# GpSimd's second parts of weight units: four instructions of 256 columns instead of one of 1024

## The chip, the core and the metric

The kernel runs on one core of a Trainium2 chip. The core has a matrix engine (TensorE, PE in the profile; its weight loads are a row of their own, PEld), three elementwise engines (VectorE or DVE, ScalarE or ACT, GpSimd or POOL), and SyncE (SP), which issues the transfers from DRAM. The engines run side by side, each in its own order, and wait for each other by semaphores. The metric is the device time of one launch in microseconds (us).

## The reference, cut to what matters

One layer of a hybrid decoder over 2048 prompt tokens and 32 sample tokens, with 1024 features:

```
h = rmsnorm(x, g_mix); proj = h @ w_in              # 1024 x 2560, split in u, q, k, v, g
ssm = S5 state space of u (scan over tokens, GELU, GLU)
ret = retention of q, k, v, g (4 heads, rotary phases, chunks of 128)
x = x + concat(ssm, ret) @ w_out
x = x + memory_attend(rmsnorm(x, g_xattn), mk, mv, w_mq, w_mo)   # 256 memory tokens, 4 heads
h = rmsnorm(x, g_mlp)
x = x + square(relu(h @ w_up)) @ w_down             # 1024 x 4096 and back
y = rmsnorm(x, g_final)
```

All of it is float32. The memory's keys and values are made from the prompt memory by two further products.

## The kernel before, in words

The tokens are worked on in four blocks of 512 (the second with the 32 sample tokens beside it). Each block goes through the mixers, the output projection, the memory attention and the MLP. Weights stream from DRAM in units of 128 x 1024 float32 numbers (`raw`), over and over, once per block.

A float32 product is made as three products in the faster float32r format. For this each weight unit gets two parts, `whl[:, 0]` (the first part: the number in float32r) and `whl[:, 1]` (the second: what is left), and the activations likewise (`act`, `z`, `actl`). ScalarE makes the first part of a weight unit with a copy. VectorE or GpSimd makes the second part: it subtracts the first part from `raw`. This second part is what the change touches. It is made in the function `lo` inside `split_unit`. Which engine makes it is set by a table (`SET`, read by `ve`) or, for some units, by the smaller of two guesses. Matrix products read the unit in steps of 128 columns or more (`fm`: for each step of 128, the passes first x first, first x second, second x first), so the first product that needs the second part stands two or three places behind the first product of a unit.

The memory's key and value products write `kt` and `vt`; with these two further sets of weights are multiplied in (products named `dn<-kt,whl` and `dn<-whl,vt`), between the first block's mixers and its attention.

The order of instructions is not written out by hand. The class `Order` runs a main sequence of weight units and, in between, chains (state space, retention, norms) as generators. A model of the engines (`Model`, with a start cost and a cost per column for each elementwise engine; 140 ns and 2.11 ns for GpSimd) guesses when each instruction ends, and a chain goes on when the guess says that its inputs are there. So every instruction that is added to an engine moves the guesses, and with them the places at which chains come in between on all engines. All instructions of the elementwise engines pass through one helper, which is why they all have line 197 in the profile; matrix products have line 445, transposes 449.

In the rows below: `pkd`, `psc`, `pkv`, `po` and `pt` are retention's products, `Sv`, `scs`, `kr` and `qr` what they read; `py`, `vr` and `vi` are the state space's products, `Yr`, `Yi` and `t` its scans and their results; `rst`, `rsy` and `parts` are the short chain that makes the reciprocal root of a norm.

Of the kernel before, what the change touches and what calls it, by code (L numbers as in the profile page):

```python
# [18 lines left out]
P = 128  # L19
# [40 lines left out]
class Item:  # L60
    """A piece of the main sequence: a weight unit to load and what to do with it, or a call."""

# [12 lines left out]
class Model:  # L75
    """Guesses when each engine does what it is given, from the operands and the engines' rates."""

# [10 lines left out]
    def where(self, ap):  # L88
        """First and last partition and element, outermost stride, elements within it."""
        dims = [tuple(d) for d in ap.ap]  # L90
        p0 = p1 = 0
        lo = ap.offset
        if ap.space != DRAM:
            row, n = dims.pop(0)
            if row:
                p0, lo = divmod(lo, row)
            p1 = p0 + n
        dims = sorted((abs(s), n) for s, n in dims if n > 1)
        w = 1 + sum((n - 1) * s for s, n in dims[:-1])
        s, n = dims[-1] if dims else (1, 1)  # L100
        return p0, p1, lo, lo + (n - 1) * s + w, s, w
# [81 lines left out]
class Engine:  # L183
    """An engine whose instructions the model sees."""

# [15 lines left out]
class Either:  # L201
    """An instruction for the engine that SET names, or for the one that the model has done with it first."""

# [27 lines left out]
class Order:  # L231
    """Emits the program in the order of the tensor engine's time: a main sequence of weight units,
    and chains that come in between when their latencies have passed."""

# [4 lines left out]
    def spawn(self, gen, *aps):  # L239
        """A chain, from when the tiles are ready."""  # L240
        s = Side(gen, max(self.clock, self.model.ready(*aps)))
        self.sides.append(s)
        return s

    def resume(self, s):
        """A chain goes on when the engines have done what it gave them, or some time later, or when tiles are ready."""
        last, self.model.last = self.model.last, 0.0
        try:
            x = next(s.gen)
            s.last = self.model.last + (SET[x] if isinstance(x, str) else 200)  # L250
            if x is None or isinstance(x, str):
                s.wake = max(self.clock, s.last)
            elif isinstance(x, list):
                s.wake = max(self.clock, self.model.ready(*x))
            else:
                s.wake = max(s.wake, self.clock) + x
        except StopIteration:
            s.done = True
            self.sides.remove(s)
        self.model.last = max(last, self.model.last)  # L260

    def work(self, out, ins, cost):
        """A matrix product."""
        self.clock = max(self.clock, self.model.after("PE", [out], ins)) + cost
        self.model.note("PE", [out], ins, self.clock)
# [63 lines left out]
def tile_decoder_step(ctx: ExitStack, tc: tile.TileContext, ins: dict, outs: dict):  # L329
# [93 lines left out]
    def split_unit(raw, eng, pool=None, tag="whl", bufs=NW):  # L423
        """Both float32r parts of a unit, [P, 2, 1024]."""
        hl = (pool or wpool).tile([P, 2, 1024], F32R, tag=tag, name=tag, bufs=bufs)
        A.activation(hl[:, 0, :], raw, AF.Copy)

        def lo():
            e = eng or min((V, G), key=lambda e: max(model.free[e.key], model.ready(hl)) + 1024 * Model.RATE[e.key][1])
            e.tensor_tensor(out=hl[:, 1, :], in0=raw, in1=hl[:, 0, :].bitcast(F32), op=ALU.subtract)  # L430
        return hl, lo
# [29 lines left out]
    def split(dst, src, scale=None):  # L461
        """dst[:, 0] + dst[:, 1] = src (* scale) in float32r parts."""
        split_first(dst, src, scale)
        split_rest(dst, src, scale)

    def rsqrt(pool, tag, x, n):
        """x ** -0.5 on [P, n]."""
        y = pool.tile([P, n], F32, tag=tag + "y", name="rsy")
# [14 lines left out]
    def fm(w, acts, t, out, nk=KT, order=None):  # L483
        """One 128-row tile of W^T X: w(k, s) gives lhsT; fills out with (PSUM tile, column, columns)."""
        for o, n in pieces(t) if isinstance(t, int) else t:
# [9 lines left out]
    def stats(pool, acc, cols, eps_tag):  # L495
        """(mean square + eps) ** -0.5 by token; cols: list of (lhsT slice of acc, rows, further summands)."""
        n = len(cols)
# [20 lines left out]
    def spread(dst, rs, t, last=None, row=None):  # L518
        """dst[p, token] = rs[token]: rs column i holds tokens i*128.., `last` the sample column; row: space for 512 tokens."""
        nt = min(t, BT) // P  # L520
# [23 lines left out]
    def s5_setup(sp):  # L544
        """The tables and matrices of the state space, four pairs of groups at a time, into DRAM."""
        cnt = [0]
# [26 lines left out]
        def turns(*gens):  # L573
            """One instruction of each in turn."""
            gens, n = list(gens), 0
# [8 lines left out]
        def poly(x, cs, out):  # L584
            """((cs[0] x + cs[1]) x + ...) x, without a constant term."""
            ts(x, cs[0], None, mul, out=out)
            yield
            for c in cs[1:]:
                stt(out, c, x, add, mul, out=out)
                yield  # L590
# [117 lines left out]
        yield from turns(angle(), quadrant(), exp(lr, mag), sine(), cosine(), recip())  # L708
        # a = mag (cos + i sin), and the parts of a product with it
        a, b_ = tt(cst[:, 0:2], both(st_["ev"]), mul), tt(cst[:, 1:3], both(st_["odd"]), mul)  # L710
# [62 lines left out]
        def products(out, n, x, y, tab, neg):  # L773
            """out gets the real and imaginary parts of (x + i y) tab, the latter with neg for tab."""
            SH = [P, 4, n, 16]
# [51 lines left out]
    def all_tables(jt, fhf, fl, hpi):  # L827
        """cos and sin of the angles' multiples."""
        W = [P, 4, 129]
# [21 lines left out]

    # The sample tokens go with block SB up to the queries, then through the MLP with the next one.
    blk = [dict(b=b, sample=b == SB, t=TM_ if b == SB else BT, c0=b * BT + (NS if b > SB else 0),
# [22 lines left out]
    def fill(side, lst, n):  # L876
        """Runs a chain until lst has n entries."""
        while len(lst) < n and not side.done:
            od.resume(side)

    def fm_item(src, view, acts, t, done, nk=KT, eng=None, order=None, tag="lo"):
        """One weight unit: view(hl) gives a list of w(k, s); done(i, out) takes the i-th result."""
        def fn(hl):
# [14 lines left out]

# [1 line left out]
    M = {}  # L900
# [36 lines left out]
    def mem_items():  # L937
        """Keys and values of the memory, and the query and output weights with them multiplied in."""
        T_ = {"k": [], "v": []}
# [71 lines left out]

# [1 line left out]
    RING = {"qr": (0, 1), "kr": (2, 3), "cosr": (4,), "sinr": (5,), "rb": (6,), "gate": (7, 10), "tmp": (8, 9),  # L1013
# [30 lines left out]
    def mix_take(B, k, x, rest=None):  # L1044
        """One row tile of the input: its parts and squares; `rest` comes in between."""
        t = B["t"]
# [53 lines left out]
    def first_load(B, units, side):  # L1100
        """The first block's input with the weights of its first product, and a chain in between."""
        B["acts"], xs, raws, hls, half = [], [], [], [], 512
# [424 lines left out]
    def ret_keep(B, h, i, x):  # L1527
        """Sets the sample columns of a query, key or gate tile aside."""
        if B["sample"]:
# [163 lines left out]

# [1 line left out]
    def rk(shape, tag, bufs=1, dt=F32):  # L1695
# [31 lines left out]
    def normed_split(B, o, gain, hs, t):  # L1727
        """Its first part; gives what does the second."""
        hs[o] = a = act() if o < KT - 4 or "rest" not in pool else zact()
# [160 lines left out]
    def sample_keep(B):  # L1890
        """Sets the sample columns of the normalised input aside."""
        M["hss"] = t = rk((P, 2, NB, 2, NS), "pmk", 1, F32R)[:, 0]
# [6 lines left out]
    def sample_items():  # L1899
        """The sample tokens' queries, their attention over the caches, and its output weights."""  # L1900
        held["zps"] = True
# [47 lines left out]
    def sample_rows(Z):  # L1949
        """The sum of both parts of the rows in PSUM, and its transpose, tile by tile."""  # L1950
        ps = Z["ps"]
# [92 lines left out]
    def mo_last(B, u, ahead):  # L2044
        """The last two heads, row tile by row tile."""
        keep = []
# [326 lines left out]
```

## Time and profile before

| | |
|---|---|
| median of 3 runs | 3097.52 us (3088.29 to 3099.51) |
| span of the profiled execution | 3086.3 us |
| PE busy in it | 2950.1 us, 96% |
| DVE busy | 1826.7 us, 59% |
| POOL busy | 1189.3 us, 39% |
| ACT busy | 1005.9 us, 33% |

The profiled execution has only its span, from the first to the last instruction; what a launch takes beside that is not listed for it. The span is 2.0 us under the fastest of the three runs and 11.2 us under their median. A busy matrix engine is not yet one that works at its peak, but idle time of PE is time in which nothing of the main work goes on, and here it is 136 us of the span.

### The profile page before, as it was taken

Reading aid. Unit: us, or ns where it says so; the run is one execution under the profiler, and the core shown is the slowest. Engines: PE = TensorE matmul, PEld = TensorE weight load, DVE = VectorE, ACT = ScalarE, POOL = GpSimd, SP = SyncE. Lnnn points to the kernel's source line nnn. Section 1 sums busy time; section 2 is a strip of 40 time slices with the busy share of each in tenths; the row PEclk is TensorE's granted clock in tenths of the full one; section 3 lists DMA queues with packets and bytes.
Section 4 is the critical chain, followed back from the end, with each engine's and each line's share of the span. In section 5 each row is a group of like instructions: output and inputs, shape, how many; then the busy total and the mean of one; then the engine's idle time right before and its main releaser. Section 6 shows DMA issues by size and latency. Waiting matters only on the chain.

```text
span 3086.3 us, 42360 instructions
## 1 busy us (share of the span) xinstructions
PE 2950.1 (96%) x16676; PEld 2566.3 (83%) x16676; DVE 1826.7 (59%) x3079; ACT 1005.9 (33%) x1440; POOL 1189.3 (39%) x764
## 2 busy tenths in 40 slices
PE   8898899998989999999999999999999999999998
PEld 6788787877877878887987888788999998878887
DVE  9968868679686563334465555655533344554334
ACT  4432232322444332223343333343322223332222
POOL 5424434244454243333524333361523325153333
PEclk9999999999999999999999999999999999999999
DMA  5452252342674322224324444542222233222222
GB/s 150 136 176 97 97 166 96 130 145 72 220 251 157 105 89 96 96 96 140 117 83 138 142 146 147 190 145 89 83 89 89 86 133 119 89 89 96 96 96 75
DMA packets 138950, 374.32 MB, mean 121 GB/s; under 512 B 18656, under 2 KB 39808, under 8 KB 138752
## 3 DMA queue, kind: packets, MB, share of 16 engines
q1 hardware_dynamic: 138176, 371.10, 36.1%
q8 instruction: 131, 2.15, 0.3%
q14 instruction: 67, 0.55, 0.1%
q10 hardware_dynamic: 576, 0.52, 0.1%
HBM read 334.17 MB, written 37.40 MB: 120 GB/s over the span
## 4 chain that ended last, share of the span: by engine, by line
PE 61%; DVE 2%; issue 1%; DMA 1%; ACT 1%; POOL 1%; SPq 0%; POOLq 0%; ACTq 0%; DVEq 0%
PE dn L445 54%; PE sc L445 6%; PE zps L445 1%; DMA raw<-in_w_down 1%; DVE rst L197 1%; ACT whl L197 0%; PE ptp L449 0%; DVE rsy L197 0%; DVE act L197 0%; DVE pmk L197 0%; PE st L445 0%; DVE whl L197 0%; POOL whl L197 0%; POOL act L197 0%; PE sp L445 0%
## 5 line engine op out<-in xcount | busy, mean ns | idle before, releaser
L445 PE MATMUL dn<-act,whl 128*128 128x512 f32 (+2 forms) x4704 | 914.2, 348 | 8.4 <-DVE whl L197 7.4
L445 PE MATMUL dn<-actl,whl 128*128 128x512 f32 (+2 forms) x4656 | 917.3, 356 | 5.1 <-DVE x L197 4.9
L445 PEld LDWEIGHTS dn<-actl,whl 128*128 128x128 f32 x4656 | 767.5, 188 | 134.6 <-issue 3.8
L445 PEld LDWEIGHTS dn<-act,whl 128*128 128x128 f32 x4704 | 753.4, 190 | 116.5 <-DVE whl L197 8.4
L197 POOL TENSOR_TENSOR whl<-raw,whl 128x1024 fp32r<-128x1024 f32 x225 | 559.1, 2487 | 549.1 <-ACT whl L197 536.1
L197 ACT ACTIVATE whl<-raw 128x1024 fp32r<-128x1024 f32 (+1 forms) x505 | 522.7, 1045 | 655.5 <-PE dn L445 445.2
L197 DVE TENSOR_TENSOR x<-dn,x 128x512 f32<-128x512 f32 (+2 forms) x496 | 291.1, 605 | 429.0 <-PE dn L445 428.3
L197 DVE TENSOR_TENSOR whl<-raw,whl 128x1024 fp32r<-128x1024 f32 (+1 forms) x280 | 401.7, 1441 | 165.2 <-ACT whl L197 152.9
L445 PE MATMUL dn<-z,whl 128*128 128x512 f32 (+1 forms) x2160 | 434.9, 353 | 0.0
L445 PEld LDWEIGHTS dn<-z,whl 128*128 128x128 f32 x2160 | 353.7, 188 | 56.8 <-issue 1.1
L197 POOL TENSOR_TENSOR actl<-sq,actl 128x512 fp32r<-128x512 f32 (+1 forms) x128 | 171.3, 1339 | 485.8 <-DVE sq L197 471.5
L197 DVE SCALAR_TENSOR_TENSOR relu<-dn,rb 128x512 f32<-128x512 f32 (+1 forms) x160 | 91.6, 589 | 324.7 <-PE dn L445 317.3
L197 ACT ACTIVATE actl<-relu 128x512 fp32r<-128x512 f32 (+1 forms) x128 | 82.0, 641 | 515.9 <-DVE relu L197 515.9
L445 PE MATMUL dn<-whl,act 128*128 128x512 f32 x768 | 200.1, 408 | 10.8 <-ACT whl L197 6.1
L197 POOL TENSOR_TENSOR acc<-acc,relu 128x512 f32<-128x512 f32 (+2 forms) x77 | 107.4, 1395 | 249.9 <-ACT relu L197 247.8
L445 PEld LDWEIGHTS dn<-whl,act 128*128 128x128 f32 x768 | 165.8, 253 | 34.4 <-ACT whl L197 6.8
L197 DVE TENSOR_TENSOR sq<-relu 128x512 f32<-128x512 f32 (+1 forms) x128 | 90.2, 704 | 14.8 <-POOL actl L197 2.3
L445 PE MATMUL sc<-whl,act 128*128 128x256 f32 x576 | 81.0, 293 | 15.0 <-ACT p L197 9.2
L445 PEld LDWEIGHTS sc<-whl,act 128*128 128x128 f32 x576 | 76.0, 200 | 16.1 <-ACT p L197 9.9
L197 DVE SCALAR_TENSOR_TENSOR act<-x,small,act 128x512 fp32r<-128x512 f32 (+2 forms) x76 | 70.0, 928 | 27.0 <-ACT act L197 26.9
L445 PE MATMUL sc<-whl,z 128*128 128x256 f32 x576 | 80.7, 291 | 0.0
L197 ACT ACTIVATE act<-x,small 128x512 fp32r<-128x512 f32 (+2 forms) x76 | 52.9, 699 | 78.9 <-DVE x L197 55.0
(317 smaller groups left out, 2743.9 us busy)
## 6 DMA issues: line engine op xcount, KB each, us to landing
raw<-in_w_up SPq DMA_DIRECT2D x128, 512.0 KB, 3.5
raw<-in_w_down SPq DMA_DIRECT2D x128, 512.0 KB, 3.5
raw<-in_w_out SPq DMA_DIRECT2D x32, 512.0 KB, 3.5
raw<-wq_d SPq DMA_DIRECT2D x32, 512.0 KB, 3.6
raw<-wo_d SPq DMA_DIRECT2D x32, 512.0 KB, 3.5
x<-in_xT SPq DMA_DIRECT2D x48, 256.0 KB, 4.3
pm<-pm_d SPq DMA_DIRECT2D x16, 768.0 KB, 4.6
tab<-tab_d SPq DMA_DIRECT2D x16, 516.0 KB, 3.5
```

The lines of the kernel that those rows point to most:

```text
L197: return f(*args, **kw)
L445: T.matmul(out, lhsT, rhs, start=start, stop=stop)
```

## The change

`lo` now makes the second part, where GpSimd makes it, in four instructions of 256 columns, one behind the other. VectorE's stay as they were, one of 1024 columns. The choice of engine by guesses is unchanged, and so are the model's rates; the model books each of the four instructions with its own start cost.

```
         def lo():
             e = eng or min((V, G), key=lambda e: max(model.free[e.key], model.ready(hl)) + 1024 * Model.RATE[e.key][1])
-            e.tensor_tensor(out=hl[:, 1, :], in0=raw, in1=hl[:, 0, :].bitcast(F32), op=ALU.subtract)
+            n = 256 if e is G else 1024
+            for i in range(0, 1024, n):
+                e.tensor_tensor(out=hl[:, 1, i:i + n], in0=raw[:, i:i + n], in1=hl[:, 0, i:i + n].bitcast(F32), op=ALU.subtract)
...
```

The rest of the diff takes comments out. Lines behind the change move down by two, so 445 and 449 are 447 and 451 in the changed kernel.

GpSimd's order in the first block, where units stand between retention's `qr` and `kr`, before:

```order
L197 TENSOR_TENSOR qr<-qr,tmp 128x512
L197 TENSOR_TENSOR whl<-raw,whl 128x1024
L197 TENSOR_TENSOR kr<-kr,tmp 128x512
L197 TENSOR_TENSOR whl<-raw,whl 128x1024
L197 TENSOR_TENSOR z<-v_338,jt 128x516
L197 TENSOR_TENSOR pm_135<-cb_678,cb_679 64x4x5x16 x2
```

And the same place now:

```order
L197 TENSOR_TENSOR qr<-qr,tmp 128x512
L197 TENSOR_TENSOR whl<-raw,whl 128x256 x4
L197 TENSOR_TENSOR kr<-kr,tmp 128x512
L197 TENSOR_TENSOR whl<-raw,whl 128x256 x4
L197 TENSOR_TENSOR pm_135<-cb_687,cb_688 64x4x5x16 x2
L197 TENSOR_TENSOR z<-v_339,jt 128x516
```

Each unit is four instructions, `kr` stands behind the four of the unit ahead of it, and one instruction on `z` has left GpSimd for VectorE here.

PE's order where weights are multiplied into the memory's keys (`dn<-kt,whl`), with the semaphores that each product waits for (the engine's name is the semaphore's), before:

```order
L445 MATMUL dn<-kt,whl 128x256 [waits Activation_49]
L445 MATMUL dn<-kt,whl 128x256
L445 MATMUL dn<-kt,whl 128x256 [waits Pool_49]
L445 MATMUL dn<-kt,whl 128x256 x21
L445 MATMUL dn<-kt,whl 128x256 [waits DVE_49,Activation_49]
```

And now:

```order
L447 MATMUL dn<-kt,whl 128x256 [waits Activation_49]
L447 MATMUL dn<-kt,whl 128x256
L447 MATMUL dn<-kt,whl 128x256 [waits Pool_49]
L447 MATMUL dn<-kt,whl 128x256 x2
L447 MATMUL dn<-kt,whl 128x256 [waits Pool_49]
L447 MATMUL dn<-kt,whl 128x256 x11
L447 MATMUL dn<-kt,whl 128x256 [waits Pool_49]
L447 MATMUL dn<-kt,whl 128x256 x6
L447 MATMUL dn<-kt,whl 128x256 [waits DVE_49,Activation_49]
```

The third product waited for the whole second part; now it waits for a quarter of it, and later products wait for later quarters.

PE's order around the first retention head, before:

```order
L445 MATMUL dn<-act,whl 128x512 x72
L449 MATMUL pkd<-ident,kr 128x128 x4
L445 MATMUL psc<-qr,kr 128x128 x4
L445 MATMUL dn<-act,whl 128x512 x12
L445 MATMUL pkv<-tm_520,kd 128x128 x4
L445 MATMUL dn<-act,whl 128x512 x6
L449 MATMUL qt<-ident,tre_133 128x128 x4
L449 MATMUL qt<-ident,tim_134 128x128 x4
L445 MATMUL po<-tm_520,scs 128x128 x2
```

And now:

```order
L447 MATMUL dn<-act,whl 128x512 x75
L451 MATMUL pkd<-ident,kr 128x128 x4
L447 MATMUL psc<-qr,kr 128x128 x4
L447 MATMUL dn<-act,whl 128x512 x12
L447 MATMUL pkv<-tm_523,kd 128x128 x4
L451 MATMUL qt<-ident,tre_133 128x128 x4
L451 MATMUL qt<-ident,tim_134 128x128 x4
L447 MATMUL dn<-act,whl 128x512 x9
L447 MATMUL po<-tm_523,scs 128x128 x2
```

The head's first products come three weight products later, its `po` six later, and the two transposes of the state space's tables (`qt`) three earlier.

## Rows read from the trace of the kernel before

**Rows 1.** The page: span, then busy time, share and instructions of each engine.

```profile
span 3086.3 us, 42360 instructions
PE 2950.1 (96%) x16676; PEld 2566.3 (83%) x16676; DVE 1826.7 (59%) x3079; ACT 1005.9 (33%) x1440; POOL 1189.3 (39%) x764
```

**Rows 2.** Busy time by stretch: start:end length, then PE, PEld, DVE, ACT, POOL, clock, DMA.

```profile
0.00:1100.00 1100.00, 996.40 (x5811) 871.23 (x5812) 856.47 (x1657) 388.22 (x594) 448.51 (x334) 0.98 0.44 141
1100.00:3000.00 1900.00, 1878.62 (x10441) 1629.58 (x10440) 934.21 (x1353) 593.88 (x806) 707.99 (x405) 1.00 0.33 112
3000.00:3086.00 86.00, 75.03 (x427) 65.47 (x425) 36.06 (x71) 23.82 (x41) 32.76 (x26) 0.94 0.23 76
```

**Rows 3.** GpSimd's instructions by shape: count | busy, mean ns | idle before, releasers.

```profile
L197 POOL TENSOR_TENSOR whl<-raw,whl 128x1024 fp32r<-128x1024 f32 x225 | 559.1, 2487 | 549.1 <-ACT whl L197 536.1 <-issue 5.9 <-DMA raw<-in_w_up 3.6
L197 POOL TENSOR_TENSOR actl<-sq,actl 128x512 fp32r<-128x512 f32 x96 | 126.8, 1321 | 364.3 <-DVE sq L197 350.0 <-PE pp L449 10.0 <-DMA x<-cat_d 4.3
L197 POOL TENSOR_TENSOR acc<-acc,relu 128x256 f32<-128x256 f32 x7 | 5.2, 738 | 7.3 <-ACT relu L197 7.1
```

**Rows 4.** GpSimd's instructions, first 1100 us alone, the costliest group.

```profile
L197 POOL TENSOR_TENSOR whl<-raw,whl 128x1024 fp32r<-128x1024 f32 x65 | 162.2, 2497 | 109.2 <-ACT whl L197 103.1 <-issue 5.9
```

**Rows 5.** PE's waits in the first 1100 us: us in total, times, longest.

```profile
PE py L445 <- DVE t L197: 14.1, 9, 3.2
PE pkd L449 <- POOL kr L197: 13.4, 12, 2.1
PE pt L449 <- DVE scs L197: 12.8, 5, 3.9
PE dn L445 <- DVE whl L197: 12.1, 8, 2.2
PE po L445 <- DVE Sv L197: 8.0, 6, 4.0
...
PE dn L445 <- POOL whl L197: 6.5, 6, 2.2
```

**Rows 6.** PE's waits from 800 to 950 us.

```profile
PE dn L445 <- DVE whl L197: 9.2, 6, 2.2
```

**Rows 7.** Order of time, 888 to 893.5 us: start, length, instruction, [idle before, releaser].

```profile
888.79 2.35 POOL L197 TENSOR_TENSOR whl<-tm,whl 128x1024 fp32r<-128x1024 f32 x1 [2.58 <-ACT whl L197]
...
889.31 2.12 DVE L197 TENSOR_TENSOR vt<-wst,vt 128x256 fp32r<-128x256 f32 x1 [0.48 <-ACT vt L197]
...
891.20 1.22 PE L445 MATMUL dn<-kt,whl 128*128 128x256 f32 x4 [1.93 <-POOL whl L197]
```

**Rows 8.** Order of time, 1014 to 1020.5 us.

```profile
1014.86 2.39 POOL L197 TENSOR_TENSOR kv<-raw,kv 128x1024 fp32r<-128x1024 f32 x1 [7.11 <-ACT kv L197]
...
1015.93 1.34 DVE L197 TENSOR_SCALAR rsy<-ms 128x4 int32<-128x4 int32 x1
...
1017.29 2.40 POOL L197 TENSOR_TENSOR whl<-raw,whl 128x1024 fp32r<-128x1024 f32 x1
1017.30 2.40 DVE L197 TENSOR_TENSOR rst<-rsy 128x4 f32<-128x4 f32 x1
...
1020.13 0.16 DVE L197 TENSOR_TENSOR rst<-rsy 128x4 f32<-128x4 f32 x1
```

**Rows 9.** Order of time, 463.5 to 472 us.

```profile
464.29 3.68 DVE L197 TENSOR_TENSOR_SCAN Yr<-rho,carr,t 128x128 f32<-128x128 f32 x4
...
464.35 2.59 POOL L197 TENSOR_TENSOR whl<-raw,whl 128x1024 fp32r<-128x1024 f32 x1 [0.56 <-ACT whl L197]
...
468.48 1.60 DVE L197 TENSOR_TENSOR_SCAN Yi<-rho,cari,t 128x128 f32<-128x128 f32 x4
...
470.90 0.49 PE L445 MATMUL po<-Sv,qr 128*128 128x128 f32 x2 [0.75 <-DVE Sv L197]
```

**Rows 10.** The page's costliest groups: two of PE's, with idle before them.

```profile
L445 PE MATMUL dn<-actl,whl 128*128 128x512 f32 (+2 forms) x4656 | 917.3, 356 | 5.1 <-DVE x L197 4.9
...
L445 PE MATMUL dn<-z,whl 128*128 128x512 f32 (+1 forms) x2160 | 434.9, 353 | 0.0
```

## The prediction

> **What bounds the kernel now.** I read the page first, for who is busy: PE works for 2950.1 of 3086.3 us, so no more than 136 us of the span can be won without taking matrix products away, and the change takes none away [rows 1]. Next the busy time by stretch, for where those 136 us lie: 104 us in the first 1100 us, 21 us in the following 1900 and 11 us in the last 86 [rows 2]. In the first stretch DVE is busy for 856 of 1100 us and POOL for 449; in the middle, where the MLPs are, PE is nearly never idle. So this kernel is bound by PE, and a change to GpSimd's work can act at two places: in the first 1100 us, through what PE waits for there, or by making PE slower, anywhere. Then PE's waits in that stretch: the long ones are for results of DVE (`t` 14.1, `scs` 12.8, `whl` 12.1, `Sv` 8.0 us), then `kr` from GpSimd (13.4 us), and 6.5 us in six waits for a second part that GpSimd makes [rows 5]. Last the order of time around three of those waits [rows 7 to 9].
>
> **Part 1: what four instructions cost on GpSimd.** One of 1024 columns takes 2487 ns, one of 512 takes 1321, one of 256 (another operation's, with the same two inputs from SBUF) 738 [rows 3]. These lie on a line: 1166 ns for 512 columns, so 583 for 256, and 155 ns to start. Four of 256 take 4 x 738 = 2952 ns, 465 ns more than one of 1024. Over 225 units that is 105 us more of POOL, which then is busy for 1294 us, 42% of the span. POOL waits 536 us for ScalarE's first parts ahead of just these units [rows 3], so this time fits into waits that are there. It reaches PE only where something stands right behind a unit in GpSimd's order and PE waits for that. `kr` is the one that counts, and it waits 0.465 us longer if its inputs are ready before the unit ends. PE waited twelve times for it [rows 5], so the bounds are 0 (if each `kr` waits for DVE's product ahead of it and not for the unit) and 12 x 0.465 = 5.6 us. I take 1 us.
>
> **Part 2: what the first quarter gives.** PE waited for the whole second part and now waits for a quarter: the first is there after 0.74 us instead of 2.4 to 2.5, 1.7 us earlier, and the last comes 0.47 us later. At 888.79 us a unit starts on POOL, and PE stands still for 1.93 us until it ends [rows 7]; with a quarter the product could start after 0.74 us, and the next quarters come every 0.74 us. The six waits in the first stretch sum to 6.5 us with a longest of 2.2 [rows 5], so a gain of 1.7 us each leaves at most 0.5 in the longest; all six could shrink to some 1 us. What is late next there is VectorE: in the same 150 us PE waits 9.2 us for VectorE's second parts [rows 6], and a PE that comes 1.9 us earlier to such a product waits that much longer for it. So the gain lies between 0 and 5.5 us. I take 3.
>
> **Part 3: three more waits of PE for each unit.** They are nearly always satisfied when PE comes to them. The trace holds such waits already: each of the units behind the 4656 `dn<-actl` and 2160 `dn<-z` products has at least one for each part, and PE's idle time ahead of those groups is 5.1 us, 4.9 of it one late result, and 0.0 us [rows 10]. So I put them at 0. If the 0.2 us left over there belonged to the waits alone, the 708 new ones (three for each of some 236 units, those made from `kv` and `tm` included) would still cost under 1 us.
>
> **Part 4: GpSimd against VectorE.** This is where a large term could hide. At 1015.93 us a DVE instruction on 4 columns takes 1.34 us and the next one 2.40, while the same `rst` takes 0.16 a little later; the long ones end when POOL's instructions of 1024 columns end [rows 8]. At 464.29 us four scans take 3.68 us beside a POOL unit, four others without one 1.60: 2.08 us lost, 0.5 us less than the whole unit [rows 9]. So these DVE instructions stood still for the rest of POOL's running instruction. The Trainium skill says the same ("SBUF — State Buffer", section "SBUF: two separate sides"): the port pair that VectorE and GpSimd share is an exclusive lock, held for a whole instruction, and the loser blocks. The trace agrees, by the 2.40 us above. By that rule alone, shorter instructions would cut each stall to the length of a quarter, which is the first rival.
>
> I don't take that cut as a gain, because of what follows the stalled instruction. At 464 us VectorE has four scans ready, one behind the other, and POOL got its turn as soon as the instruction ahead of them was done. With quarters a scan waits some 0.6 us, runs 0.40, then the next quarter has its turn, and so on: four scans pay four times 0.6, or 2.4 us, where they paid 2.08. The chain at 1015 us has eight short instructions and meets two units, so it would pay for all remaining quarters as well. Only where VectorE has one or two instructions ready does it come out sooner. And the unit itself ends later, by each scan that went in between. For a busy VectorE, then, the time that both engines hold the port is what it was plus 0.465 us for each unit, that is at most 65 x 0.465 = 30 us in the first stretch [rows 4]; for an idle one it is a gain of up to 1.7 us at each stall. VectorE is busy for 78% of that stretch [rows 2], so I expect both. Of the loss I take one unit in eight as on PE's path (65 / 8 x 0.465 = 4 us), of the gain 3 us: together +1.
>
> **Part 5: the moved order.** On PE's queue side products move by some places, first where retention's first head comes three products later. A place is about 0.2 us (917.3 us for 4656 products [rows 10]), so three to six places are 0.6 to 1.2 us, about as long as one of PE's twelve waits for `kr`. No row of before has a price for such a move; the bounds are that those waits, 13.4 us [rows 5], vanish because the products behind them come later, or that as much is lost at other places. I take 0, the middle.
>
> **The sum.** +1 (part 1) - 3 (part 2) + 0 + 1 + 0 = -1 us on the span of 3086.3. That execution's span stands 11.2 us under the median of the runs shown, and a change of the span is a change of the time, so 3097.5 - 1, rounded to **3096 us**. What a measurement of this kernel can tell from no change is about 0.5%, 15 us.
>
> **The rivals.**
>
> *VectorE is set free.* Each stall of up to 2.4 us becomes at most 0.74, if VectorE goes on for good after it. For it: PE's four longest waits for DVE results in the first stretch are 14.1 + 12.8 + 12.1 + 8.0 = 47.0 us [rows 5], and two of the three places that I looked at begin with such a stall. Against it: VectorE's queue is mostly full there, and then the quarters take turns with it. If half of the 47.0 us go, and part 2 gives its 5.5, the time is 3097.5 - 23.5 - 5.5 = 3068 us. If a third goes it is 3076.
>
> *The quarters get stuck (slower).* A unit that ran through in 2.5 us now has four places at which it must wait for VectorE. With a scan of 0.40 us in each of three gaps it ends after 2.95 + 1.2 = 4.2 us, 1.7 us later than before; with instructions of 1 us more. Whatever stands behind it on GpSimd (`kr`, the state space's `t`) and the unit's last columns are late by that. It decides where VectorE is dense, so in the first 1100 us with their 65 units [rows 4]. If one unit in five puts its 1.7 us on PE's path, that is 13 x 1.7 = 22 us: 3120 us. Against it: POOL has 109 us of idle time ahead of these units [rows 4] and the planner asks for each unit well before PE needs it, since only six times did PE wait for one.
>
> *The planner's new order costs.* Chains come in at other places, and their latencies were met at the old ones only to a microsecond or two. With `pkd`'s and `pt`'s waits grown by half (13.4 + 12.8, half is 13 us [rows 5]) the time is 3111 us.
>
> **How the numbers follow.** The forecast, no change that can be told, has 0.50, with its own range of 3083 to 3111. VectorE set free has 0.25, since its mechanism is seen in the trace and only the yield is doubtful. The stuck quarters have 0.15 and the new order with a loss 0.10; the latter lands half of the time within the bound. So: faster by over 0.5% 0.25, within 0.50 + 0.05 = 0.55, slower 0.15 + 0.05 = 0.20. The range must reach into both sides: from 3070, between the two prices of the first rival, to 3119, just under the price of the second; I leave out about 0.1 on either end.
>
> **What would show it.** POOL's units at 4 x 0.7 to 0.8 us and some 1290 us busy (part 1). PE's wait for POOL's `whl` in the first 1100 us down from 6.5 us to about 1, with the wait for DVE's `whl` grown or unchanged (part 2). PE still with no idle time in the MLPs (part 3). Scans beside a unit that are each 0.5 to 0.6 us longer, instead of one that is 2 us longer, and DVE's busy time within some 30 us of 1826.7 (part 4). The prediction is wrong if DVE's busy time falls by 50 us and more and PE's idle time in the first 1100 us, 104 us now, falls with it, or if that idle time grows by more than 15 us.

## The result, and the profile after

The changed kernel takes **3063.97 us** (3057.99 to 3065.02, 4 runs) against 3093.97 us before (3088.29 to 3099.51, also 4 runs, one more than were known at the prediction): the ratio is 0.9898, with a 95% interval of 0.9877 to 0.9918. It is some 30 us faster, where no change was forecast; the time lies 6 us under the range's lower end. What happened is the first rival, VectorE set free, whose price stood at 3068 us. The sign that the prediction had set for being wrong came too: VectorE's busy time fell by more than 50 us, and PE's idle time in the first 1100 us fell with it.

The page after: span, then busy time of each engine [rows 1].

```profile
span 3055.8 us, 43238 instructions
PE 2944.5 (96%) x16676; PEld 2561.3 (84%) x16676; DVE 1767.3 (58%) x3088; ACT 1007.1 (33%) x1440; POOL 1314.5 (43%) x1463
```

PE does the same products, and its idle time went from 136 to 111 us (span less busy time), which is 25 of the 30.5 us between the two spans. The other 5.6 us are PE's busy time: 16676 products in 2944.5 us for 2950.1. The mean granted clock (1.0 is its upper level, 2.4 GHz, and 0.5 its lower, 1.2 GHz) was 0.988 for 0.987 in the two profiled executions; over all runs it was 0.982 to 0.987 before and 0.986 to 0.988 in the changed kernel. What part of the gain comes by the clock, no run takes apart. GpSimd is busy for 125 us more. VectorE, whose work was not touched but for nine instructions that the planner moved to it, is busy for **59 us less**. That is the row to see first: an engine that does the same work in less time had been held up in its instructions. Here it is by stretch [rows 2]; in the first two columns behind the length are PE and PEld, then DVE.

```profile
0.00:1100.00 1100.00, 1015.05 (x5911) 883.86 (x5912) 830.05 (x1692) 399.28 (x609) 515.97 (x545) 0.98 0.45 143
1100.00:3000.00 1900.00, 1884.92 (x10475) 1637.09 (x10474) 914.27 (x1340) 592.19 (x800) 773.59 (x884) 1.00 0.34 112
```

PE gets through 100 more products in the first 1100 us (5911 for 5811), and its idle time there is 85 us instead of 104. The pieces themselves, GpSimd's costliest group by shape [rows 3]:

```profile
L197 POOL TENSOR_TENSOR whl<-raw,whl 128x256 fp32r<-128x256 f32 x896 | 692.7, 805 | 510.8 <-ACT whl L197 494.3 <-DMA wo_d<-wst 6.9 <-issue 4.5
```

And PE's waits in the first 1100 us, with their total, count and longest [rows 5]:

```profile
PE pt L451 <- DVE scs L197: 13.9, 7, 4.4
PE py L447 <- DVE t L197: 12.2, 9, 3.2
PE pkd L451 <- POOL kr L197: 11.4, 10, 2.1
...
PE dn L447 <- DVE whl L197: 6.1, 5, 3.3
...
PE dn L447 <- POOL whl L197: 4.4, 6, 0.9
...
PE po L447 <- DVE Sv L197: 2.8, 2, 1.4
```

The wait for GpSimd's second parts became shorter, as it should (6.5 to 4.4 us). The larger part is on VectorE's side: `whl` 12.1 to 6.1, `Sv` 8.0 to 2.8, though single rows move with the order as well. Over the whole run, all rows of this view added up, PE waited 85 us for VectorE's results before and 67 now, 21 and 19 us for GpSimd's, and 23 and 19 us for ScalarE's.

### The profile page after: what moved, and what is told of

Same layout as the page of the kernel before. It is cut to its first block, busy times and chain, and to the rows that moved or that the text cites. A ratio compares the mean times of both kernels' runs of the same rounds, so it can differ in the third digit from the quotient of the medians.

```text
span 3055.8 us, 43238 instructions
## 1 busy us (share of the span) xinstructions
PE 2944.5 (96%) x16676; PEld 2561.3 (84%) x16676; DVE 1767.3 (58%) x3088; ACT 1007.1 (33%) x1440; POOL 1314.5 (43%) x1463
## 4 chain that ended last, share of the span: by engine, by line
PE 65%; DVE 1%; issue 0%; DMA 0%; ACT 0%; POOL 0%; POOLq 0%; SPq 0%; ACTq 0%; DVEq 0%
PE dn L447 57%; PE sc L447 6%; PE zps L447 1%; DVE rst L197 1%; PE ptp L451 0%; PE st L447 0%; DVE rsy L197 0%; DMA raw<-in_w_down 0%; DVE act L197 0%; PE sp L447 0%; POOL x L197 0%; DVE mx L197 0%; ACT x L197 0%; DVE stage L197 0%; DVE ms L197 0%
## 5 line engine op out<-in xcount | busy, mean ns | idle before, releaser
L197 POOL TENSOR_TENSOR whl<-raw,whl 128x256 fp32r<-128x256 f32 x896 | 692.7, 805 | 510.8 <-ACT whl L197 494.3
```

What stands on the lines that cost most here:

```text
L197: return f(*args, **kw)
```

## The experiments

Three theories were tried. A: VectorE's instructions stall for a quarter of a unit instead of for the rest of a whole one. B: PE starts on the first quarter. C: the planner's new order. The first four kernels take the change apart; each is compared with runs of the kernel before on its own chip. Where a kernel keeps "the order of before", the planner is told of one instruction of 1024 columns (`model.done(...)` once) and the pieces are issued past it, so each engine's instructions stand as before.

**The order alone.** The planner books four, one is issued:

```
-                e.tensor_tensor(out=hl[:, 1, i:i + n], in0=raw[:, i:i + n], in1=..., op=ALU.subtract)
+                model.done(e.key, "tensor_tensor", [hl[:, 1, i:i + n]], [raw[:, i:i + n], ...])
+            e.eng.tensor_tensor(out=hl[:, 1, :], in0=raw, in1=hl[:, 0, :].bitcast(F32), op=ALU.subtract)
```

> The changed kernel's order on every engine (the planner still books four instructions), but GpSimd's second part made in one instruction of 1024 columns. The changed kernel was 30 us faster. Theory A (VectorE stalls for a quarter, not for a whole unit) and theory B (PE starts on the first quarter) both expect no gain here: ratio 0.997 to 1.006, DVE busy within 15 us of 1826.7. Theory C (the planner's new order makes the gain) expects all of it: ratio 0.988 to 0.993.

Measured: 3092.2 us against 3097.37, ratio 0.9981 (0.9971 to 0.9991). The new order is worth 0.2% of the 1.0%; C falls as the main cause. VectorE is busy for 1807.3 us, 19 less than before, where at most 15 either way was expected: the order alone takes some stalls away too, and little time comes of it.

**The pieces alone**, order of before:

```
+            model.done(e.key, "tensor_tensor", [hl[:, 1, :]], [raw, hl[:, 0, :].bitcast(F32)])
             n = 256 if e is G else 1024
             for i in range(0, 1024, n):
-                e.tensor_tensor(...)
+                e.eng.tensor_tensor(...)
```

> Four instructions of 256 columns with the order of before on every engine (the planner books one of 1024). A and B expect the gain of the changed kernel or nearly so: ratio 0.988 to 0.993, DVE busy some 1767 us. C expects no gain: 0.997 to 1.003.

Measured: 3064.89 us, ratio 0.9895 (0.9882 to 0.9908), all of the gain. Its page:

```profile
span 3061.0 us, 43236 instructions
PE 2944.0 (96%) x16676; PEld 2563.0 (84%) x16676; DVE 1778.7 (58%) x3079; ACT 1006.2 (33%) x1440; POOL 1328.4 (43%) x1475
```

VectorE has exactly the 3079 instructions of before, in the same order, and is busy for 48 us less. So the time that it lost was time inside its instructions.

**The quarters interleaved.** Each of the four instructions takes 32 columns of every 128, so each product needs all four and PE waits for the last, as it waited for the whole:

```
...
+            o, x, h = (t.rearrange("p (m c) -> p m c", m=8) for t in (hl[:, 1, :], raw, hl[:, 0, :].bitcast(F32)))
+            for i in range(0, 128, 32):
+                e.eng.tensor_tensor(out=o[:, :, i:i + 32], in0=x[:, :, i:i + 32], in1=h[:, :, i:i + 32], op=ALU.subtract)
```

> The order of before, four instructions for each unit, but each takes 32 columns of every 128, so that PE waits for the last of the four as it waited for the whole unit, while VectorE's stalls can be cut as with quarters. A expects most of the gain of the pieces alone: ratio 0.989 to 0.995, DVE busy below 1790 us, PE's wait for GpSimd's second parts in the first 1100 us not below 6.5 us. B expects none of it: 0.998 to 1.005, since the second part then comes 0.4 us later.

Measured: 3068.61 us, ratio 0.9906 (0.9885 to 0.9928). PE's wait for these second parts in the first 1100 us rose, as it should, from 6.5 us before to 8.9:

```profile
PE dn L451 <- POOL whl L436: 8.9, 8, 2.1
```

and yet nearly the whole gain is there, with VectorE busy for 1780.0 us. So B isn't needed: the difference to the pieces alone is 0.1%, within the intervals' overlap, and these runs leave B some 0.4% at the most. A stands.

**Eight pieces**, order of before (`n = 128`):

> The order of before, eight instructions of 128 columns. By the line through the shapes of before one takes 155 + 292 = 447 ns, a unit 3.6 us. A: stalls of VectorE shorter once more, but more of them; ratio 0.985 to 0.995, DVE busy at or below that of four. B: the first eighth comes only 0.3 us sooner than a quarter: same as four pieces to 0.2%. If GpSimd's added time begins to matter, it is slower than four.

Measured: 3059.49 us, ratio 0.9876 (0.9862 to 0.9889). DVE is busy for 1753.9 us, 73 less than before. Two rows show what it costs, GpSimd's pieces and PE's wait for them in the first 1100 us:

```profile
L433 POOL TENSOR_TENSOR whl<-raw,whl 128x128 fp32r<-128x128 f32 x1800 | 855.2, 511 | 457.0 <-ACT whl L197 447.4 <-issue 5.9 <-POOL actl L197 3.3
```

```profile
PE dn L448 <- POOL whl L433: 11.9, 12, 1.9
```

**Sixteen pieces**, order of before (`n = 64`):

> The order of before; sixteen instructions of 64 columns. By the line of shapes one takes 155 + 146 = 300 ns, a unit 4.8 us, POOL over 55% busy. If only the length of VectorE's stall counts, ratio 0.983 to 0.988, below that of eight (0.9876). If GpSimd's own time now reaches PE (its wait for GpSimd's second parts was 5.1 us with four and 11.9 with eight), it is slower than eight: 0.988 to 0.996.

Measured: 3111.64 us, ratio 1.0054 (1.0036 to 1.0072): slower than before the change, and than either expectation. A unit now keeps GpSimd busy for 1160.4 / 225 = 5.2 us, where a whole took 2.5, and GpSimd's results come late, over the whole span:

```profile
L433 POOL TENSOR_TENSOR whl<-raw,whl 128x64 fp32r<-128x64 f32 x3600 | 1160.4, 360 | 375.4 <-ACT whl L197 364.5 <-issue 5.2 <-DVE whl L433 3.5
```

```profile
PE dn L448 <- POOL whl L433: 24.7, 13, 3.6
PE pkd L452 <- POOL kr L197: 22.5, 12, 5.6
```

As in the slower rival of the prediction, GpSimd's unit ends late, at four times the number of pieces that I had thought it would take. The reason is mostly another one: undisturbed pieces of 64 columns follow each other every 0.28 us, so sixteen take 4.5 us without any wait for VectorE, and only the other 0.7 us can be turns with it.

With the order of before, PE's waits over the whole run, by the engine whose result ended them, tell why the time first falls and then rises:

| pieces | PE waits for VectorE | for GpSimd | for ScalarE | VectorE busy | mean clock in all runs | time |
|---|---|---|---|---|---|---|
| 1 | 85 us | 21 us | 23 us | 1826.7 us | 0.982 to 0.987 | 3097 us |
| 4 | 67 us | 21 us | 23 us | 1778.7 us | 0.986 to 0.988 | 3064.89 us |
| 8 | 49 us | 33 us | 19 us | 1753.9 us | 0.988 to 0.989 | 3059.49 us |
| 16 | 47 us | 71 us | 13 us | 1784.0 us | 0.981 to 0.983 | 3111.64 us |

From one piece to eight PE waits less and less for VectorE; from eight to sixteen it gains 2 us there and loses 38 us behind GpSimd. Waits are not the whole of it: between the profiled executions with eight and sixteen, 31 of the 53 us are idle time of PE and 21 its busy time, for the same products at a lower clock.

**Where the gain is made.** Quarters for some units only, order of before; the condition is put on the unit's name (`tag`):

```
...
-            n = 256 if e is G else 1024
+            n = 256 if e is G and mine in ("l_mk", "l_mv", "l_wq", "l_wo") else 1024
```

> The order of before; four instructions of 256 columns only for the 18 of GpSimd's 237 units that hold weights of the memory's key and value products. In the traces the changed kernel runs ahead by 4 us at 796 us, by 18 at 1005 and by 31 at the end. If the stalls of VectorE cost most where PE follows VectorE closely (the memory stretch), 18 units give 10 to 16 us: ratio 0.994 to 0.997. If each unit is worth the same, they give 18/237 of 32 us, 2.4 us: 0.998 to 1.000.

> The order of before; four instructions only for the 57 units of the mixers' products (and the few units without a name of their own, eight in the memory attention among them). VectorE is busiest in the mixers and PE waits there for its results. If the gain of 32 us is made where PE follows VectorE, and the memory's 16 to 18 units made 8 us of it, these should make more than the remaining 164 units together: 12 to 20 us, ratio 0.9935 to 0.996. If the turns that I wrote of eat the gain wherever VectorE's queue is full, 0.998 to 1.002.

> The order of before; four instructions only for the 164 units of the output projections, the memory attention and the MLPs. PE is nearly never idle there, save at the borders of blocks, where short chains of VectorE stall twice for a unit. Expected 4 to 10 us: ratio 0.997 to 0.9987. If each unit were worth the same, 22 us: 0.993.

| units with quarters | number | ratio (95%) | gain of 3097 us | per unit |
|---|---|---|---|---|
| memory's keys and values | 16 | 0.9974 (0.9965 to 0.9984) | 8.1 us | 0.50 us |
| mixers (and eight of the memory attention) | 57 | 0.9953 (0.9936 to 0.9970) | 14.6 us | 0.26 us |
| all others: output projections, attention, MLPs | 164 | 0.9969 (0.9953 to 0.9985) | 9.6 us | 0.06 us |
| all | 237 | 0.9895 (0.9882 to 0.9908) | 32.5 us | 0.14 us |

The three gains sum to 32.3 us. (The memory's units number 16; the first of the three expectations says 18.) Each gain is known to some 3 to 5 us either way. So a unit of the memory's products, where PE follows VectorE closely, is worth at least three times one of the last group, and eight times by the medians. For the 57 units the gain is inside what was expected, for the memory's just under it, for the others at its upper end (0.9969, where 0.997 to 0.9987 had been said).

**MLP's second parts in quarters too.** On top of the pieces alone:

```
-                        E("x_r3").tensor_tensor(out=a[:, 1, :t], in0=r2[:, :t], in1=..., op=ALU.subtract)
+                        model.done("G", "tensor_tensor", [a[:, 1, :t]], [r2[:, :t], ...])
+                        for i in range(0, t, t // 4):
+                            c = slice(i, i + t // 4)
+                            G.eng.tensor_tensor(out=a[:, 1, c], in0=r2[:, c], in1=a[:, 0, c].bitcast(F32), op=ALU.subtract)
```

> Four pieces and the order of before, and in addition the MLP's second parts (actl, 128 instructions of 512 or 544 columns on GpSimd) in quarters. VectorE's busy time should fall by 20 to 40 us more, as its instructions stall behind actl too. As PE is busy throughout the MLPs, no time should come of it: ratio within 0.003 of that of four pieces alone (0.9895). If VectorE's stalls are worth the same wherever they stand, 0.978 to 0.984.

Measured: 3064.51 us, ratio 0.9897 (0.9879 to 0.9914), that of the pieces alone. The stretch from 1100 to 3000 us, first of the pieces alone, then of this kernel:

```profile
1100.00:3000.00 1900.00, 1885.41 (x10480) 1636.60 (x10479) 914.43 (x1340) 592.29 (x802) 775.56 (x884) 1.00 0.35 112
```

```profile
1100.00:3000.00 1900.00, 1885.22 (x10472) 1634.05 (x10471) 880.52 (x1349) 590.91 (x800) 921.64 (x1261) 1.00 0.35 112
```

VectorE is freed of 34 us more, and PE's 1885 us stay. Stalls that PE doesn't wait for were worth nothing that these runs can tell.

**Looking for a faster version.** Eight pieces booked by the planner (the changed kernel with `n = 128`), and eight pieces but four for the memory's units:

> The changed kernel with 128 columns in place of 256: eight instructions, each booked by the planner with its start cost, so a third order. If the pieces carry the gain and the order some 0.2%, as the first four runs say, ratio 0.984 to 0.990, and faster than the changed kernel. If an order that books 8 x 140 ns for each unit spreads the chains badly, 0.990 to 0.997.

> The order of before; eight instructions of 128 columns, but four for the memory's 16 units, where PE waited 11.9 us for GpSimd's second parts with eights and 5.1 with fours. If those waits are lost time, 3 to 6 us faster than eighths throughout (0.9876): ratio 0.985 to 0.987. If PE waits for VectorE there as soon as it stops waiting for GpSimd, the same as eighths: 0.987 to 0.989.

Measured: 0.9914 (0.9899 to 0.9928) for the first, 0.9872 (0.9855 to 0.9888) for the second. The planner's order for eights costs 0.4% against the old order, where its order for fours gained 0.2% when run alone: a new order moves the time by some tenths of a per cent either way. The second, at 3059.52 us the fastest kernel along with eight pieces throughout (3059.49), is not told apart from it, as the second branch of its expectation says. Its trace has the reason: in the first 1100 us PE's wait for GpSimd's second parts fell from 11.9 to 5.1 us, the one for VectorE's second parts rose from 6.3 (3.7 + 2.6) to 9.5 (6.6 + 2.9), and the one for `t` from 13.8 to 16.0. Another wait took the place. The ratios of these two kernels with the old order, 0.9876 and 0.9872, are below the changed kernel's 0.9898, with intervals that just overlap.

## Why the prediction was wrong

**Part 4 failed, in its price for the turns.** The prediction said: "four scans pay four times 0.6, or 2.4 us, where they paid 2.08", and that for a busy VectorE the time that both engines hold the port stays what it was, plus 0.465 us a unit. The same four scans after the change, with the unit beside them and four scans without one:

```profile
467.64 2.90 DVE L197 TENSOR_TENSOR_SCAN Yr<-rho,carr,t 128x128 f32<-128x128 f32 x4
...
467.70 3.36 POOL L197 TENSOR_TENSOR whl<-raw,whl 128x256 fp32r<-128x256 f32 x4 [0.56 <-ACT whl L197]
...
471.04 1.60 DVE L197 TENSOR_TENSOR_SCAN Yi<-rho,cari,t 128x128 f32<-128x128 f32 x4
```

They lose 2.90 - 1.60 = 1.30 us, not 2.4, and before it was 2.08 [rows 9]. The turns are there, just as described. A single scan and the quarter beside it:

```profile
468.84 0.89 DVE L197 TENSOR_TENSOR_SCAN Yr<-rho,carr,t 128x128 f32<-128x128 f32 x1
```

```profile
468.59 0.85 POOL L197 TENSOR_TENSOR whl<-raw,whl 128x256 fp32r<-128x256 f32 x1
```

Each was longer by its wait: the scan 0.89 for 0.45 us undisturbed, the quarter 0.85 for 0.74. A scan and a quarter one after the other would take 0.45 + 0.74 = 1.19 us; the quarters behind this one started at 469.41 and 470.22, so a turn of both takes 0.81. That is 0.38 us less than the two recorded lengths. Some 0.1 of it is found behind an instruction of the same engine too (undisturbed scans follow each other every 0.38 us, quarters every 0.70), and some 0.27 us are left: **part of the recorded length of a GpSimd instruction does not shut VectorE out**, and with four instructions this part comes four times. I had the 0.5 us between the stall and the unit's length in the rows (2.08 and 2.59, [rows 9]) and didn't ask what four of them would do. And the first scan, which had begun before the unit, did not pay at all, so three pay 0.43 us each, not four 0.6. The unit in turn ends after 3.36 us, not after the 4.2 that the second rival gave it, and over the run a unit keeps GpSimd busy for 692.7 / 224 = 3.1 us; so that rival did not come.

**The rest of that part held only for chains of small instructions.** The norm's chain in the changed kernel:

```profile
991.06 2.81 POOL L197 TENSOR_TENSOR kv<-raw,kv 128x256 fp32r<-128x256 f32 x4 [3.51 <-ACT kv L197]
...
993.24 0.66 DVE L197 TENSOR_TENSOR rst<-rsy 128x4 f32<-128x4 f32 x1
993.83 2.82 POOL L197 TENSOR_TENSOR whl<-raw,whl 128x256 fp32r<-128x256 f32 x4
993.93 0.66 DVE L197 SCALAR_TENSOR_TENSOR rst<-rst,ms 128x4 f32<-128x4 f32 x1
994.63 0.66 DVE L197 SCALAR_TENSOR_TENSOR rsy<-rst,rsy 128x4 f32<-128x4 f32 x1
995.32 0.67 DVE L197 TENSOR_TENSOR rst<-rsy 128x4 f32<-128x4 f32 x1
996.01 0.65 DVE L197 SCALAR_TENSOR_TENSOR rst<-rst,ms 128x4 f32<-128x4 f32 x1
996.70 0.16 DVE L197 SCALAR_TENSOR_TENSOR rst<-rst 128x4 f32<-128x4 f32 x1
```

Five instructions pay 0.5 us each (0.66 for 0.16), 2.5 us in all, where two paid 1.18 + 2.24 = 3.4 [rows 8]. Here the turns eat most of the gain, and the quarters keep their pace (2.82 us, four times 0.70).

Over the whole run I compared each VectorE instruction's length with what its kind takes undisturbed (the 10th percentile of its name and shape), and put the excess down to the GpSimd instruction that ran when it began. Behind weight units of before that gives some 80 stalls with 134 to 139 us, 1.7 us each, by where small excesses are cut off; in the kernel with the pieces alone some 194 stalls with 88 to 90 us, 0.45 us each. There are 2.4 times as many stalls, not four times, and each is a quarter as long. Where the prediction put "+1" for this part, VectorE was freed of 48 us (busy time with the pieces alone), and PE waited 18 us less for it. How the freed time divides between queues that were full and single instructions that were alone was not measured apart.

**The lock** was the right guide here. The Trainium skill ("SBUF — State Buffer", section "SBUF: two separate sides") has the pair of ports locked for a whole instruction, so shorter instructions mean shorter stalls. The traces agree as to the stall's scale (2.24 us behind a whole, 0.50 behind a quarter). The scan and the quarter above, whose turn is 0.38 us shorter than their two lengths, show that a recorded length is more than the time for which the other is shut out.

**Part 1 held in kind.** One piece takes 805 ns on average and 719 at the least, for 738 predicted; POOL is busy for 1314.5 us, 20 more than said. Half of the units take no more than 2.84 us, under the 2.95 said; the mean is 3.1, since some wait for VectorE, as the one above does. With four pieces hardly any of it is seen at PE: its wait for `kr` went from 13.4 to 11.4 us in the changed kernel, and to 14.4 with the pieces alone. With sixteen it is 22.5.

**Part 2 was too hopeful and mattered little.** The six waits shrank to 4.4 us, not 1. At 873.62 us of the changed kernel a unit takes 3.52 us because VectorE takes turns with it, and PE waits twice for its pieces:

```profile
873.62 3.52 POOL L197 TENSOR_TENSOR whl<-tm,whl 128x256 fp32r<-128x256 f32 x4 [2.83 <-ACT whl L197]
...
874.40 0.62 PE L447 MATMUL dn<-kt,whl 128*128 128x256 f32 x3 [0.30 <-POOL whl L197]
...
875.97 2.50 PE L447 MATMUL dn<-kt,whl 128*128 128x256 f32 x19 [0.94 <-POOL whl L197]
```

The wait for VectorE's second parts, which I had named as what is late next, halved in the changed kernel. The pieces don't do that by themselves: with the order of before it stays at 6.6 + 5.1 = 11.7 us, for 12.1 before, "grown or unchanged" as the prediction said.

```profile
PE dn L448 <- DVE whl L433: 6.6, 6, 2.8
...
PE dn L448 <- DVE whl L197: 5.1, 3, 4.2
```

**Part 3 held.** In the stretch from 1200 to 1400 us PE has no idle time, before and after, with three waits more for each unit. **Part 5**: the order alone is worth 0.2% and not 0, and with the pieces it is not seen (0.9898 with it, 0.9895 without).

**The range.** Its lower end stood at 3070, between half and a third of four of PE's waits for VectorE. The gain wasn't confined to those four, which fell by 12 us, from 47.0 to 35.0 (by 6, to 41.2, with the pieces alone): 9.6 us came from the 164 units of the output projections, the attention and the MLPs, where I had counted nothing. So the rival's price came near the measured time partly by luck: its mechanism came, but of its 23.5 us from the four waits 12 came, and of its 5.5 from part 2 some 2; the rest lay where its sum doesn't look. The rival had a quarter of the chance with its mechanism plain in the rows; what held me back was an argument about turns whose price I hadn't taken from them.

## What to carry to other kernels

When an engine's instructions grow and shrink with what another engine does, look for the longest instruction of the other one and cut it: the stall is cut with it, and the added start costs fall on the engine that has time. Count what a turn costs from one pair in the trace before arguing that turns give the gain back. Stop cutting when PE begins to wait for the engine with the pieces: here eight pieces were as good as or better than four, and sixteen were slower than one. It pays most at units where the main engine follows the stalled one: 0.50 us for each in the memory's products, and 0.06 for each in the output projections, the attention and the MLPs taken together.

## What the runs showed of the hardware that was not expected

Where a VectorE and a GpSimd instruction take turns, a turn is shorter than their two recorded lengths: by 0.38 us for a scan of 0.45 us and a quarter of 0.74, and by 0.2 us for the norm's instructions (0.16 + 0.74, every 0.70). So splitting a GpSimd instruction hides part of its added start cost behind VectorE's work. A piece of 64 columns takes 360 ns on average and one of 128 511, both over the 300 and 447 that the line through longer shapes gives; half of them take no more than 322 and 460. Four pieces of 32 columns out of every 128 cost GpSimd what four pieces of 256 columns in a row do: 693.4 us for 900 of them, and 692.7 for 896.
